# A hybrid encoder layer on one core: the order of the first stage's loads, x blocks and first products

## The chip, the cores and the metric

The kernel runs on one core of a Trainium2 chip. TensorE (PE) multiplies matrices and transposes, VectorE (DVE) and ScalarE (ACT) work elementwise, GpSimd (POOL) does small vector work, and SyncE's queue (SP) asks for most transfers. Each engine takes its own instructions in order and waits on semaphores for the others. The metric is the device time of one execution in microseconds; of several runs the median is given.

## What is computed

One layer of a streaming encoder, for a prompt of 512 frames and a sample of 64 frames, with width D = 2048, all in fp32:

```
mod = silu(c) @ w_ada + b_ada;  sh1, sc1, g1, sh2, sc2, g2 = split(mod, 6)
h = rmsnorm(x, norm1) * (1 + sc1) + sh1
proj = h @ w_in          # columns of GLA (q, k, v, r, low rank) and of DeltaNet (q, k, v, g, beta, alpha)
mix = [gated linear attention | gated DeltaNet](proj) @ w_out
x = x + g1 * mix
h = rmsnorm(x, norm2) * (1 + sc2) + sh2
x = x + g2 * (silu(conv3(gate) + b) * val @ w_down),  gate, val = split(h @ w_up)
y = rmsnorm(x, final_norm)
```

The DeltaNet part needs for each head and block the decays exp(cumsum(g)) with g from the alpha columns, and the inverse of a unit triangular 64 x 64 matrix. New states are returned too.

## The kernel before

Activations are kept transposed: 16 k-tiles of 128 features by two halves of 288 frames (256 of the prompt and 32 of the sample). For fp32 products each operand is split into two parts, high and low, and `mm6` (L555, matmuls at L564 and L566) makes six matmuls for one k-tile and one column of 128 weights: high by high, low by high, high by low, each for both halves. A column's sum lies in a PSUM tile named g, of which there are two (`pgt`, L579).

`head` (from L654) is the first stage. Its parts:

- The constants and small vectors are loaded and transposed (`load_vectors`, L593, transposes at L625).
- `modulation(g)` (L710) makes scale (mi = 1) and shift (mi = 0) for four k-tiles: for each, four chunks of four k-tiles of w_ada, of which each comes in two loads of 512 KB into tiles named hraw (five buffers, L720), with eight matmuls on quarters of the array (L724; two of them count as one step k). It ends with a copy from PSUM (L727), transposes (L157), a reduction (L730). It is a generator; each `yield` stands before a chunk.
- `x_block(b)` (L681) loads one block of x (four of the prompt, one of the sample), takes squares on ACT (L688), the norm by a power on POOL (L1725), scales on DVE (L692), transposes on PE (L697) and copies on ACT into xT (L700, L704). The five blocks are called between the chunks of modulation(0).
- Then for each group g of four k-tiles: the narrow weights (66 columns of low rank, beta, alpha, `narrow_w`) are loaded; four h tiles are made by `split_mod` (scale and shift on DVE at L586, high part hh on ACT at L587, low part hl on DVE at L588); each has four narrow products (L878); then come six columns (EARLY) of the in projection, in pairs by `pair_w` (L771: two loads of 256 KB each into a raw tile, high part on ACT at L778, low part on DVE at L779), and for each column four mm6 and `sum_early` (first group a copy on ACT, L788; later an addition on DVE, L793). modulation(g + 1) moves on by one step after each narrow product and each column.

When `head` is done, `narrow` (L880) starts the gate chain: the narrow sums are copied out (na) and turned (L891), beta and the logarithm ln follow on ACT and DVE, two products with a triangle of ones (L926) give cum, further ones (L935, L951) the last values and rows, which go through DRAM (gd, L954) and come back broadcast to all partitions (gb, L349). From this the decays are made, POOL selects the triangles, and together with keys (kt, norm on POOL at L1725) the matrix m, whose 16 x 16 blocks go through DRAM (d, L372 and L378) to POOL's inverse (`inverse16`, L367). PE meanwhile goes on with further columns of the in projection by mm6; L249, L255 and L157 are PE's later uses of that chain.

The order of the work is set by a scheduler of the framework: the program is written in one sequence, a priority can be raised in a block (`high_priority`, used in `pair_w`), and each engine then gets its fixed queue. Loads all stand on SP, in order, and each waits for its buffer. Buffers are reused in rotation (`bufs`), by which a load or product waits for the last reader.

## Time and profile before

| | us |
|---|---|
| median of 3 runs | 2925.44 (2918.93 to 2926.12) |
| the profiled execution | 2921.86 |
| its span | 2920.1 |
| first mm6 product (timeline) | 65.81 |
| last product of the head ends (chain) | 193.25 |
| POOL's first inverse starts (timeline) | 237.19 |

In the profile, L12 is a line of the kernel; "x6" counts instructions in a row, and "[1.40 <-ACT hh L587]" says that the engine stood idle for 1.40 us and that ACT's writing of hh ended it. "PEclk" is the clock granted to PE, in tenths. A group's row in the view by lines gives the busy time in total and the mean of one in ns. The waits of an engine are listed with their total, their number and the longest. DMA rows give what moved in a stretch.

### The profile page before, as it was taken

What the parts mean: (1) busy time and instruction counts of PE and PEld (TensorE: products, weight loads), DVE (VectorE), ACT (ScalarE), POOL (GpSimd) and SP (SyncE); (2) the same over time, 40 slices, a digit from 0 to 9 for tenths busy, and PEclk for the clock granted to TensorE, in tenths of its full rate; (3) what the DMA queues carried; (4) which work ended last, traced back from release to release, by engine and by line L of the source; (5) the groups of instructions that cost most, each with busy time, mean ns of one, the idle gap of its engine ahead of it and who ended that gap; (6) DMA issues with size and microseconds to landing.
All of it is one profiled execution on the core that took longest, in us unless ns stands there. A gap on an engine that the chain in (4) does not pass through costs nothing.

```text
span 2920.1 us, 52016 instructions
## 1 busy us (share of the span) xinstructions
PE 2823.8 (97%) x20964; PEld 2734.4 (94%) x20964; DVE 2051.2 (70%) x3299; ACT 1182.5 (40%) x2032; POOL 311.7 (11%) x513
## 2 busy tenths in 40 slices
PE   6999989999899999999999999999999999999998
PEld 3688889999899998999999999999999999999997
DVE  3368666777568787578888888888888855555555
ACT  4234534555454343255444444444444421222223
POOL 0005141222200000000111111111111100000000
PEclk8999999999999999999999999999999999999999
DMA  8865544555444548633333334333333553323221
GB/s 267 283 204 150 161 133 138 149 150 161 135 131 144 155 118 231 184 119 96 106 111 107 102 104 116 109 99 107 109 109 106 181 185 97 119 96 120 80 81 66
DMA packets 535444, 395.53 MB, mean 135 GB/s; under 512 B 59657, under 2 KB 465412, under 8 KB 535204
## 3 DMA queue, kind: packets, MB, share of 16 engines
q1 hardware_dynamic: 527860, 390.54, 44.7%
q8 instruction: 165, 2.70, 0.4%
q10 hardware_dynamic: 7344, 1.67, 0.3%
q14 instruction: 75, 0.61, 0.1%
HBM read 356.47 MB, written 35.67 MB: 134 GB/s over the span
## 4 chain that ended last, share of the span: by engine, by line
PE 80%; DVE 6%; POOL 4%; issue 4%; DMA 3%; ACT 2%; SPq 1%; ACTq 0%; POOLq 0%; DVEq 0%
PE g L564 26%; PE g L566 13%; PE bank L1388 11%; PE bank L1387 11%; PE bank L1389 11%; POOL m L1725 3%; DVE acc L850 1%; PE bank L724 1%; PE bank L157 1%; PE bank L441 1%; DVE wl L652 1%; DVE ca L990 1%; DVE m L1710 1%; ACT m L1710 1%; DMA d<-m 1%
## 5 line engine op out<-in xcount | busy, mean ns | idle before, releaser
L1388 PE MATMUL bank<-slot,wh 128*128 128x290 f32 x2464 | 737.3, 299 | 0.0
L1387 PE MATMUL bank<-slot,wh 128*128 128x290 f32 x2464 | 733.2, 298 | 0.0
L1389 PE MATMUL bank<-slot,wl 128*128 128x290 f32 x2464 | 728.2, 296 | 0.0
L564 PE MATMUL g<-slot,wh 128*128 128x288 f32 x3168 | 552.7, 295 | 0.2 <-DVE slot L1157 0.2
L564 PE MATMUL g<-hh,wh 128*128 128x288 f32 x2048 | 476.6, 313 | 1.0 <-ACT wh L651 1.0
L1389 PEld LDWEIGHTS bank<-slot,wl 128*128 128x128 f32 x2464 | 470.6, 191 | 0.0
L1388 PEld LDWEIGHTS bank<-slot,wh 128*128 128x128 f32 x2464 | 468.7, 190 | 0.1
L564 PEld LDWEIGHTS g<-slot,wh 128*128 128x128 f32 x3168 | 464.5, 188 | 0.7 <-DVE slot L1157 0.5
L1387 PEld LDWEIGHTS bank<-slot,wh 128*128 128x128 f32 x2464 | 463.6, 188 | 0.1
L651 ACT ACTIVATE wh<-raw 128x1024 fp32r<-128x1024 f32 x215 | 227.6, 1058 | 539.1 <-PE g L564 507.0
L564 PE MATMUL g<-hl,wh 128*128 128x288 f32 x2048 | 445.1, 298 | 0.0
L566 PE MATMUL g<-hh,wl 128*128 128x288 f32 x2048 | 443.7, 297 | 0.0
L1157 DVE SCALAR_TENSOR_TENSOR slot<-g,mod,slot 128x512 f32<-128x512 f32 (+1 forms) x448 | 201.6, 491 | 268.5 <-PE g L566 267.7
L564 PEld LDWEIGHTS g<-hh,wh 128*128 128x128 f32 x2048 | 328.4, 191 | 20.8 <-issue 16.3
L850 DVE SCALAR_TENSOR_TENSOR acc<-aw,ct,acc 128x512 f32<-128x512 f32 x480 | 337.7, 750 | 10.2 <-DMA aw<-in_w_ada_dram 10.2
L566 PE MATMUL g<-slot,wl 128*128 128x288 f32 x1584 | 342.6, 295 | 0.0
L566 PEld LDWEIGHTS g<-hh,wl 128*128 128x128 f32 x2048 | 331.6, 190 | 6.2 <-issue 6.2
L564 PEld LDWEIGHTS g<-hl,wh 128*128 128x128 f32 x2048 | 332.4, 190 | 3.6 <-issue 3.5
L652 DVE TENSOR_TENSOR wl<-raw,wh 128x1024 fp32r<-128x1024 f32 x215 | 262.6, 1222 | 64.6 <-ACT wh L651 64.0
L1334 ACT ACTIVATE wh<-raw 128x1024 fp32r<-128x1024 f32 x176 | 186.2, 1058 | 224.2 <-PE bank L1388 182.3
L566 PEld LDWEIGHTS g<-slot,wl 128*128 128x128 f32 x1584 | 256.1, 188 | 0.0
L1335 DVE TENSOR_TENSOR wl<-raw,wh 128x1024 fp32r<-128x1024 f32 x176 | 215.3, 1223 | 54.0 <-ACT wh L1334 54.0
(351 smaller groups left out, 3102.2 us busy)
## 6 DMA issues: line engine op xcount, KB each, us to landing
raw<-in_w_up_dram SPq DMA_DIRECT2D x176, 512.0 KB
aw<-in_w_ada_dram SPq DMA_DIRECT2D x128, 512.0 KB
raw<-in_w_in_dram SPq DMA_DIRECT2D x100, 512.0 KB
raw<-in_w_down_dram SPq DMA_DIRECT2D x88, 512.0 KB
hraw<-in_w_ada_dram SPq DMA_DIRECT2D x64, 512.0 KB
raw<-in_w_out_dram SPq DMA_DIRECT2D x32, 512.0 KB
slot<-actd SPq DMA_DIRECT2D x44, 288.0 KB
actd<-v SPq DMA_DIRECT2D x44, 256.0 KB
```

Of the source, the lines that this page charges most:

```text
L564: T.matmul(ps[:, h if bank is None else bank, :n], wh, x[:, h, :n], start=f, stop=False)
L566: T.matmul(ps[:, h if bank is None else bank, :n], wl, ah[:, h, :n], start=False, stop=stop)
L651: nc.scalar.activation(hi[:, :n_], raw[:, :n_], AF.Copy)
L652: nc.vector.tensor_tensor(lo[:, :n_], raw[:, :n_], hi[:, :n_].bitcast(F32), op=ALU.subtract)
L850: V.scalar_tensor_tensor(acc[s], w[:, k], col, acc[s], op0=ALU.mult, op1=ALU.add)
L1157: self.nc.vector.scalar_tensor_tensor(x1[:, :, z], ps[:, :, c], gain[:, q:q + 1], x1[:, :, z], op0=ALU.mult, op1=ALU.add)
L1334: self.nc.scalar.activation(hi, src, AF.Copy)
L1335: self.nc.vector.tensor_tensor(lo, src, hi.bitcast(F32), op=ALU.subtract)
L1387: T.matmul(ps, wh[:, j], hi, start=(c < 3 and j == 0), stop=False, skip_group_check=True)
L1388: T.matmul(ps, wh[:, j], lo, start=False, stop=False, skip_group_check=True)
L1389: T.matmul(ps, wl[:, j], hi, start=False, stop=(j == NPAIR - 1), skip_group_check=True)
L1725: r = f(*a, **kw)
```

## The change

The diff, cut to its core (load_vectors is split into its loads and its transposes in the same way; line numbers move by 1 to 30 in head and by 87 or 88 behind it, so L564 is L565, L724 is L754, L878 is L966, L926 is L1014, L935 is L1023, L1725 is L1812):

```diff
+N_HRAW, HRAW_AHEAD = 8, 3
...
-    def split_mod(self, x, s, b, hh, hl, tmp):
+    def split_mod(self, x, s, b, hh, hl, tmp, other=False):
 
         nc = self.nc
         for c, q in ((slice(0, HP), 0), (slice(HP, HT), 1)):
+            if other:
+                nc.scalar.activation(tmp[:, :, c], x[:, :, c], AF.Identity, bias=b[:, q:q + 1], scale=s[:, q:q + 1])
+                continue
             nc.vector.tensor_scalar(tmp[:, :, c], x[:, :, c], s[:, q:q + 1], b[:, q:q + 1], op0=ALU.mult, op1=ALU.add)
...
+        def x_load(b):
+            n = P if b < 4 else TS
+            xt[b] = [slot() for _ in range(4)]
+            for q in range(4):
+                f = slice(q * 512, (q + 1) * 512)
+                nc.sync.dma_start(xt[b][q][:n], i["x_prompt"][0, b * P:(b + 1) * P, f] if b < 4 else i["x_sample"][0, :, f])
+
+        def x_square(b):
+            n = P if b < 4 else TS
+            ms[b] = pool.tile([P, 8], F32, tag="ms4", bufs=2, name=self.name("ms4"))
+            for q in range(4):
+                A.activation(junk[:n], xt[b][q][:n], AF.Square, scale=float(D) ** -0.5, accum_out=ms[b][:n, q:q + 1])
+
+        def x_scale(b):
+            n, m = P if b < 4 else TS, ms[b]
+            V.tensor_reduce(m[:n, 4:5], m[:n, 0:4], axis=mybir.AxisListType.X, op=ALU.add)
+            self.rsqrt(m[:, 5:6], m[:, 4:5], 1, n)
+            for q in range(4):
+                V.tensor_scalar_mul(xt[b][q][:n], xt[b][q][:n], m[:n, 5:6])
+
+        def x_turn(b):
+            n = P if b < 4 else TS
+            per = 4 if b < 4 else 8
+            for k0 in range(0, KD, per):
+                ps = self.pgt()[:, 0]
+                for k in range(k0, k0 + per):
+                    T.transpose(ps[:, (k - k0) * n:(k - k0 + 1) * n], xt[b][k // 4][:n, k % 4 * P:(k % 4 + 1) * P],
+                                self.c["ident"][:n, :n])
+                even = k0 // per % 2 == 0
+                put = (lambda o, x: A.activation(o, x, AF.Copy)) if even else V.tensor_copy
+                if b < 4:
+                    put(xT[:, k0:k0 + per, b // 2, (b % 2) * P:(b % 2 + 1) * P], ps.rearrange("p (k t) -> p k t", k=per))
+                else:
+                    for h in range(2):
+                        put(xT[:, k0:k0 + per, h, HP:HT], ps.rearrange("p (k h t) -> p k h t", k=per, h=2)[:, :, h])
+
+        junk = slot()
+        x_load(0)
+        x_load(1)
+        self.load_consts(self.cp, LONG)
+        v_load, v_turn = self.load_vectors()
+        v_load(0)
+        v_load(1)
+        x_load(2)
+        v_turn(0)
+        v_turn(1)
...
-        def x_block(b):
-            n = P if b < 4 else TS
...
-        hraw = self.hraw = lambda: pool.tile([P, 1024], F32, tag="hraw", bufs=5, name=self.name("hraw"))
+        hraw = self.hraw = lambda: pool.tile([P, 1024], F32, tag="hraw", bufs=N_HRAW, name=self.name("hraw"))
+        todo = [(g, mi, k0) for g in range(4) for mi in (1, 0) for k0 in range(0, KD, 4)]
+        got = {}
+
+        def ada_ahead(n):
+            for j in range(len(got), min(n, len(todo))):
+                g, mi, k0 = todo[j]
+                c0 = mi * D + g * 512
+                got[j] = [hraw().rearrange("p (k n) -> p k n", k=2) for _ in range(2)]
+                for h, raw in enumerate(got[j]):
+                    k1 = k0 + 2 * h
+                    nc.sync.dma_start(raw, i["w_ada"][0, k1 * P:(k1 + 2) * P, c0:c0 + 512].rearrange("(k p) n -> p k n", p=P))
 
         def modulation(g):
+            for n in range(8 * g, 8 * g + 8):
+                _, mi, k0 = todo[n]
+                ada_ahead(n + 1)
+                if k0 == 0:
+                    ps = self.bank()
+                for k in (2, 3, 0, 1):
+                    with self.tc.issue_after(last) if k == 0 else nullcontext():
+                        T.matmul(ps[32 * k:32 * k + 32], cs[:, k0 + k], got[n][k // 2][:, k % 2], start=(k0 == 0), stop=(k0 == KD - 4))
+                    last = nc.cur_bb.bb.instructions[-1]
+                got[n] = None
+                ada_ahead(n + 1 + HRAW_AHEAD)
+                if k0 + 4 < KD:
                     yield
+                    continue
                 rw = pool.tile([P, 512], F32, tag="rw", bufs=1, name=self.name("rw"))
                 V.tensor_copy(rw, ps)
+                if g > 0:
+                    yield
...
+                if mi == 1:
+                    self.scale_mod(s1, 1, "norm1", 4 * g)
+
+        first = modulation(0)
+        ada_ahead(1)
+        x_load(3)
+        ada_ahead(2)
+        x_load(4)
+        for g in (2, 3, 4):
+            v_load(g)
+        late = [lambda: v_turn(2), lambda: v_turn(3), lambda: v_load(5), lambda: v_turn(4), lambda: v_load(6), lambda: v_turn(5), lambda: v_turn(6)]
+        for b in range(5):
+            if b == 0:
+                x_square(0)
+            x_scale(b)
+            if b < 4:
+                x_square(b + 1)
+            x_turn(b)
+            if b > 0:
+                next(first)
+        for _ in first:
+            pass
+
+        pairs = [(g, e) for g in range(4) for e in range(0, len(EARLY), 2)]
+        self.h, raws = [], {}
+
+        def w_ahead(n):
+            for j in range(len(raws), min(n, len(pairs))):
+                g, e = pairs[j]
+                raws[j] = self.pair_load([off + h * P for _, off, h in EARLY[e:e + 2]], 4 * g)
+
+        w_ahead(2)
...
+        def make(k):
+            hh, hl = self.htiles(k)
+            tmp = pool.tile([P, 2, HT], F32, tag="tmp", bufs=2, name=self.name("tmp"))
+            self.split_mod(xT[:, k], s1[:, k], self.mod[:, 0, k], hh, hl, tmp, k in (1, 3))
+            self.h.append((hh, hl))
+
+        nar = self.narrow_w(pool, 0)
         for g in range(4):
             mods = modulation(g + 1) if g < 3 else iter(())
             ks = range(4 * g, 4 * g + 4)
-            nar = self.narrow_w(pool, 4 * g)
-            for k in ks:
-                hh, hl = self.htiles(k)
-                tmp = pool.tile([P, 2, HT], F32, tag="tmp", bufs=2, name=self.name("tmp"))
-                self.split_mod(xT[:, k], s1[:, k], self.mod[:, 0, k], hh, hl, tmp)
-                self.h.append((hh, hl))
-                self.mm_narrow(k, nar[:, k % 4])
-                next(mods, None)
-            if g == 3:
-                raw = self.xr()
-                self.ps_nar = raw[:, :2 * HT].rearrange("p (h t) -> p h t", h=2)
-                V.tensor_copy(self.ps_nar[:64], ps_nar[:64, :, :HT])
-            for e in range(len(EARLY)):
-                if e % 2 == 0:
-                    w = self.pair_w([off + h * P for _, off, h in EARLY[e:e + 2]], 4 * g)
-                wh, wl = w[e % 2]
-                ps = self.pgt()
-                for k in ks:
-                    self.mm6(ps, wh[:, k % 4], wl[:, k % 4], self.h[k], k == 4 * g, k == 4 * g + 3)
-                self.sum_early(e, g, ps, accs[e])
-                next(mods, None)
+            for e in range(0, len(EARLY), 2):
+                w = self.pair_split(raws[3 * g + e // 2])
+                ps = [self.pgt() for _ in range(2)]
+                if e == 0:
+                    for k in ks:
+                        if k == len(self.h):
+                            make(k)
+                        self.mm_narrow(k, nar[:, k % 4])
+                        for j in range(2):
+                            self.mm6(ps[j], w[j][0][:, k % 4], w[j][1][:, k % 4], self.h[k], k == 4 * g, k == 4 * g + 3)
+                        if k == ks[1]:
+                            w_ahead(3 * g + 3)
+                        next(mods, None)
+                        if late:
+                            late.pop(0)()
+                    if g == 3:
+                        raw = self.xr()
+                        self.ps_nar = raw[:, :2 * HT].rearrange("p (h t) -> p h t", h=2)
+                        V.tensor_copy(self.ps_nar[:64], ps_nar[:64, :, :HT])
+                    for j in range(2):
+                        self.sum_early(j, g, ps[j], accs[j])
+                    continue
+                for j in range(2):
+                    if e == 4 and g < 3 and j == 0:
+                        nar = self.narrow_w(pool, 4 * g + 4)
+                    for k in ks:
+                        if e == 4 and g < 3 and j == 1 and k % 2 == 0:
+                            make(4 * g + 4 + k % 4 // 2)
+                        self.mm6(ps[j], w[j][0][:, k % 4], w[j][1][:, k % 4], self.h[k], k == 4 * g, k == 4 * g + 3)
+                        if k % 2 == 1:
+                            next(mods, None)
+                        if k == ks[1]:
+                            if late:
+                                late.pop(0)()
+                            if j == 0:
+                                w_ahead(3 * g + e // 2 + 3)
+                    self.sum_early(e + j, g, ps[j], accs[e + j])
...
+    def pair_load(self, offs, k0):
+
+        raw = self.raw()
+        for e, off in enumerate(offs):
+            self.nc.sync.dma_start(raw[:, e * 512:(e + 1) * 512].rearrange("p (k n) -> p k n", k=4), self.w_in(off)(k0, k0 + 4))
+        return raw
...
-        K.load_consts(K.cp, LONG)
```

What it does, in the order of the program:

- x blocks 0 and 1 are asked for ahead of the constants and vectors, block 2 behind the first vectors, 3 and 4 around chunk 1 of w_ada. The other vectors' loads and transposes move back, some into the columns (`late`).
- The block's work is cut into load, square, scale and turn; the squares of block b + 1 stand ahead of the transposes of block b, and the copies into xT alternate between ACT and DVE.
- hraw has eight buffers in place of five, and up to four chunks are asked for ahead of use.
- The loads of w_in pairs are apart from their splits and are asked for two to three pairs ahead.
- Within a group the first two columns run side by side: for each k-tile the narrow products and the products of both columns. The h tiles of the next group's first two k-tiles are made in the last column of this group. For k-tiles 1 and 3 of the first group ACT makes the scaled tile too.

Three places in the engines' queues. SP, where the first pair of w_in (raw) is asked for. Before:

```order
L685 DMA hs_461<-in_x_sample_dram 64x512
L685 DMA hs_462<-in_x_sample_dram 64x512
L720 DMA hraw_501<-in_w_ada_dram 128x2x512
L777 DMA raw_619<-in_w_in_dram 128x4x128
L720 DMA hraw_502<-in_w_ada_dram 128x2x512
L777 DMA raw_619<-in_w_in_dram 128x4x128
L720 DMA hraw_509<-in_w_ada_dram 128x2x512
L720 DMA hraw_510<-in_w_ada_dram 128x2x512
L720 DMA hraw_517<-in_w_ada_dram 128x2x512
L720 DMA hraw_518<-in_w_ada_dram 128x2x512
L867 DMA hraw_543<-in_w_in_dram 128x4x16 x2
```

and now:

```order
L744 DMA hraw_499<-in_w_ada_dram 128x2x512
L744 DMA hraw_500<-in_w_ada_dram 128x2x512
L744 DMA hraw_507<-in_w_ada_dram 128x2x512
L744 DMA hraw_508<-in_w_ada_dram 128x2x512
L744 DMA hraw_515<-in_w_ada_dram 128x2x512
L744 DMA hraw_516<-in_w_ada_dram 128x2x512
L858 DMA raw_529<-in_w_in_dram 128x4x128 x2
L858 DMA raw_532<-in_w_in_dram 128x4x128 x2
L955 DMA hraw_542<-in_w_in_dram 128x4x16 x2
L744 DMA hraw_583<-in_w_ada_dram 128x2x512
```

The first pair (raw_619 before, raw_529 now) stood within chunk 5 (counted from 0) and now stands behind chunk 10.

PE, where the second group of k-tiles begins (g is a column's sum, bank the sum of w_ada, ps_nar the narrow sum). Before:

```order
L564 MATMUL g_832<-hl_601,wh_781 128x288 x2
L566 MATMUL g_832<-hh_600,wl_782 128x288 x2
L878 MATMUL ps_nar<-hh_865,nar_859 66x288 x2
L724 MATMUL bank_876<-hraw_889,cs 32x512 x2
L724 MATMUL bank_876<-hraw_888,cs 32x512
L878 MATMUL ps_nar<-hl_866,nar_859 66x288 x2
L878 MATMUL ps_nar<-hh_877,nar_859 66x288 x2
L878 MATMUL ps_nar<-hl_878,nar_859 66x288 x2
L724 MATMUL bank_876<-hraw_888,cs 32x512
L564 MATMUL g_941<-hh_865,wh_935 128x288 x2
L564 MATMUL g_941<-hl_866,wh_935 128x288 x2
```

and now:

```order
L565 MATMUL g_811<-hl_661,wh_806 128x288 x2
L567 MATMUL g_811<-hh_660,wl_807 128x288 x2
L565 MATMUL g_901<-hh_858,wh_897 128x288 x2
L565 MATMUL g_901<-hl_859,wh_897 128x288 x2
L567 MATMUL g_901<-hh_858,wl_898 128x288 x2
L565 MATMUL g_902<-hh_858,wh_897 128x288 x2
L565 MATMUL g_902<-hl_859,wh_897 128x288 x2
L567 MATMUL g_902<-hh_858,wl_898 128x288 x2
L754 MATMUL bank_919<-hraw_756,cs 32x512 x2
L754 MATMUL bank_919<-hraw_755,cs 32x512 x2
L565 MATMUL g_901<-hh_877,wh_897 128x288 x2
```

The narrow products stood first and now stand behind the first k-tiles' products of both columns, g_901 and g_902.

PE in the columns behind the head, where the gate chain's products with ln and cum stand (g_1853 and g_1994 are the first two such columns). Before:

```order
L564 MATMUL g_1853<-hl_1193,wh_1919 128x288 x2
L566 MATMUL g_1853<-hh_1192,wl_1920 128x288
L926 MATMUL bank_1815<-ln,xr_1768 128x32
L927 MATMUL bank_1815<-ln,xr_1768 128x4
L566 MATMUL g_1853<-hh_1192,wl_1920 128x288
L564 MATMUL g_1853<-hh_1211,wh_1919 128x288 x2
L564 MATMUL g_1853<-hl_1212,wh_1919 128x288 x2
L566 MATMUL g_1853<-hh_1211,wl_1920 128x288 x2
L564 MATMUL g_1853<-hh_1230,wh_1919 128x288 x2
L935 MATMUL bank_1824<-cum,xr_1768 128x36
L936 MATMUL bank_1824<-cum,xr_1768 128x4
L951 MATMUL bank_1842<-consts_96,cum 36x128
```

and now:

```order
L565 MATMUL g_1994<-hh_955,wh_1996 128x288 x2
L565 MATMUL g_1994<-hl_956,wh_1996 128x288
L1014 MATMUL bank_1815<-ln,xr_1768 128x32
L1015 MATMUL bank_1815<-ln,xr_1768 128x4
L565 MATMUL g_1994<-hl_956,wh_1996 128x288
L567 MATMUL g_1994<-hh_955,wl_1997 128x288 x2
L565 MATMUL g_1994<-hh_986,wh_1996 128x288 x2
L565 MATMUL g_1994<-hl_987,wh_1996 128x288 x2
L1023 MATMUL bank_1824<-cum,xr_1768 128x36
L1024 MATMUL bank_1824<-cum,xr_1768 128x4
L1039 MATMUL bank_1842<-consts_193,cum 36x128
L567 MATMUL g_1994<-hh_986,wl_1997 128x288 x2
```

These products stood in the first column and now stand in the second.

71 lines of the change are left out of this document (13 added, 58 removed).

## The prediction

> **What bounds the kernel now.** I read the page first: its span, the engines' totals, the clock by slices and the shares by line of the chain that ended last.
>
> ```profile
> span 2920.1 us, 52016 instructions
> PE 2823.8 (97%) x20964; PEld 2734.4 (94%) x20964; DVE 2051.2 (70%) x3299; ACT 1182.5 (40%) x2032; POOL 311.7 (11%) x513
> PEclk8999999999999999999999999999999999999999
> PE g L564 26%; PE g L566 13%; PE bank L1388 11%; PE bank L1387 11%; PE bank L1389 11%; POOL m L1725 3%; DVE acc L850 1%; PE bank L724 1%; PE bank L157 1%; PE bank L441 1%; DVE wl L652 1%; DVE ca L990 1%; DVE m L1710 1%; ACT m L1710 1%; DMA d<-m 1%
> ```
>
> PE is busy 97% of the span, so time can be won only where PE waits or runs slowly; the clock is lowest in the first slice. POOL's 3% of the chain says that PE also waits for POOL somewhere. The change rewrites the first stage, so I read that next: as a timeline (start, length, instruction, and in brackets the idle time before it), in 5 us windows (columns: busy us of PE, PEld, DVE, ACT, POOL; granted clock; DMA share; GB/s), and its transfers up to 66 us.
>
> ```profile
> 10.16 0.63 ACT L688 ACTIVATE hs<-hs 128x512 f32<-128x512 f32 x1 [5.64 <-DMA hs<-in_x_prompt_dram]
> 14.14 0.55 POOL L1725 TENSOR_TENSOR ms<-ms,mhalf 128x1 f32<-128x1 f32 x1 [11.84 <-DVE ms L150]
> ...
> 47.42 0.54 POOL L1725 TENSOR_TENSOR ms<-ms,mhalf 64x1 f32<-64x1 f32 x1 [7.33 <-DVE ms L150]
> ...
> 50.60 0.66 ACT L704 ACTIVATE xT<-g 128x256 f32<-128x256 f32 x2 [0.19 <-PE g L697]
> ...
> 65.81 0.53 PE L564 MATMUL g<-hh,wh 128*128 128x288 f32 x2
> ...
> 71.62 0.43 PE L564 MATMUL g<-hh,wh 128*128 128x288 f32 x2
> 71.88 0.43 PE L564 MATMUL g<-hl,wh 128*128 128x288 f32 x2
> ```
>
> ```profile
> 15.00:20.00 5.00, 4.73 (x24) 3.21 (x24) 1.40 (x4) 3.22 (x7) 0.00 (x0) 1.00 1.05 406
> 50.00:55.00 5.00, 4.13 (x22) 0.96 (x20) 1.23 (x1) 2.00 (x5) 0.00 (x0) 0.52 0.28 68
> 60.00:65.00 5.00, 4.30 (x15) 2.07 (x16) 4.86 (x12) 2.73 (x4) 0.00 (x0) 0.50 0.99 318
> ```
>
> ```profile
> DMA packets 12526, 17.63 MB, mean 267 GB/s; under 512 B 1948, under 2 KB 4723, under 8 KB 12522
> hraw<-in_w_ada_dram SPq DMA_DIRECT2D x23, 512.0 KB
> ```
>
> Before the first product (65.81) the five x blocks follow one another: POOL's norm of the first is at 14.14, of the fifth at 47.42, which is 8.3 us each, and x is in place at 51.3. DMA can move 406 GB/s, yet its mean up to 66 us is 267, and 68 at 50:55: the five w_ada buffers are full and wait to be used. From 65.81 on PE is the bound, with holes only where a group of four h tiles begins (waits of PE from 65.8 to 194; total, times, longest; then the rows of the last hole):
>
> ```profile
> PE ps_nar L878 <- ACT hh L587: 4.9, 3, 2.3
> PE ps_nar L878 <- DVE hl L588: 0.8, 1, 0.8
> ```
>
> ```profile
> 171.15 0.74 PE L878 MATMUL ps_nar<-hl,nar 128*66 128x288 f32 x2 [0.76 <-DVE hl L588]
> ...
> 172.65 0.68 PE L566 MATMUL g<-hh,wl 128*128 128x288 f32 x2
> 173.13 0.68 PE L564 MATMUL g<-hh,wh 128*128 128x288 f32 x2
> ...
> 174.70 0.43 PE L564 MATMUL g<-hl,wh 128*128 128x288 f32 x2
> ```
>
> That is 5.7 us of waiting, and behind the last hole pairs start 0.48 apart (172.65, 173.13) where 0.26 is usual (71.62, 71.88): half clock from 170.9 to 174.3, 1.7 us lost. The head ends with the last product at 193.25 (the chain), and behind it stand the gate chain and the first inverse on POOL:
>
> ```profile
> 193.25 0.99 PE bank L891 x8
> ```
>
> ```profile
> 209.28 0.33 SPq L349 DMA_DIRECT2D m<-gd  x1
> 216.89 3.04 POOL L1725 TENSOR_SCALAR_AFFINE_SELECT m<-m 128x512 f32<-128x512 f32 x2 [110.49 <-ACT m L1710]
> 223.85 1.35 POOL L1725 TENSOR_TENSOR kt<-kt,mhalf 128x4 f32<-128x4 f32 x1 [3.92 <-PE bank L227]
> 237.19 0.12 POOL L1725 MEMSET m<- 32x16 f32 x1 [8.44 <-DMA m<-d]
> ```
>
> ```profile
> PE bank L157 <- DVE m L1710: 6.4, 1, 6.4
> PE bank L255 <- POOL m L1725: 6.1, 1, 6.1
> ```
>
> From 190 to 340 PE loses 12.5 us in waits on what this chain feeds. So what PE wins before 193.25 only lengthens these waits, unless the chain starts earlier too. That makes its start the second term of the sum.
>
> **The change, part by part.** No arithmetic goes away: products, transposes and loads keep their number. I use these groups (busy us, mean ns):
>
> ```profile
> L779 DVE TENSOR_TENSOR wl<-raw,wh 128x1024 fp32r<-128x1024 f32 x12 | 14.7, 1224 | 6.9 <-ACT wh L778 6.9
> L793 DVE SCALAR_TENSOR_TENSOR acc<-g,acc 128x576 f32<-128x576 f32 x17 | 12.9, 757 | 33.9 <-PE g L566 33.7
> L588 DVE TENSOR_TENSOR hl<-tmp,hh 128x576 fp32r<-128x576 f32 x16 | 11.6, 757 | 0.5
> L700 ACT ACTIVATE xT<-g 128x512 f32<-128x512 f32 x16 | 9.2, 594 | 13.2 <-PE g L697 12.8
> L727 DVE COPY rw<-bank 128x512 f32<-128x512 f32 x8 | 5.5, 692 | 36.9 <-PE bank L724 36.9
> ```
>
> *x first, overlapped.* x0 is asked for ahead of the constants, so its squares start some 4 us sooner than 10.16. The next block's squares run beside a block's transposes, and four copies on two engines take 2 x 0.69 in place of 4 x 0.59, 1 us less. I take 7 us a block in place of 8.3: x is in place at 51.3 - 4 - 5 x 1.3 = 41 at the latest, and I expect 38 to 41. The Trainium skill ("VectorE: DVE Perf Modes", Specifications) says that VectorE sits closer to SBUF and ScalarE closer to PSUM, which speaks against copies from PSUM by VectorE. The two rows agree (692 against 594), and by it alone the moved copies would cost 10 x 0.1 = 1 us; side by side they still win more.
>
> *Loads.* SP now asks for chunks 8 to 10 of w_ada (1.05 MB each, two of the 512 KB rows) ahead of the first w_in pair. Chunk 7 on needs buffers that PE frees once x is turned, near 39. Four chunks and the pair (4.7 MB) at 375 GB/s, a little under the best window, take 12.5 us, to 52 with a landing. Split on ACT and DVE (1.06 and 1.22), h tiles and narrow products put the first product at 58, 7.8 us sooner. Bounds: 54 (406 GB/s, x at 38) and 62 (318 GB/s, x at 41).
>
> *First product to head's end*, 127.4 us now. A product takes 0.133 (two rows 0.26 to 0.27 apart, two in each). Removed: waits 5.7, half clock 1.7, and of 28 runs of w_ada products (five chunks are split in two runs) five, at 1.18 each, 5.9. Added: eight narrow products that stood ahead of the first product, 1.2; half clock at the start, since PE idles between 42 and 57, 1.6. 127.4 - 5.7 - 1.7 - 5.9 + 1.2 + 1.6 = 116.9. The h tiles made early are hidden by the last column's 3.2 us of products; without that cover the old holes return.
>
> *A new wait.* Two columns side by side hold both g tiles. The second column needs the sum (0.757) of the column before, covered by the first column's six products (0.8); the third column likewise at the other end. Eight joints: at best nothing, at worst the sum stands behind a split and an hl on DVE, 0.76 + 1.22 + 0.76 - 0.8 = 1.9 each, 15 in all. DVE waited 33.7 us for PE at L793, so it is mostly early: I take 0.2 each, 1.6.
>
> Head's end: 58 + 116.9 + 1.6 = 176.5, 16.7 us sooner.
>
> *The gate chain.* Of the next columns' products, 60 stood ahead of ln's (8.0 us), now 136 do (18.1). cum, the trip through gd and the selects follow, 10.1 later against PE's work. POOL stood idle 3.92 ahead of kt, whose product on PE hasn't moved: that is the slack, and the inverse comes 10.1 - 3.9 = 6.2 later. One us more for ln, which PE may reach before it is ready, makes 7.2. Bounds: 2 (from gd's read to the selects passed 7.6 us, half of it in other work's queues, which may shrink by 4) and 11 (no slack). PE's order behind is the same, so what the inverse loses stays to the end.
>
> **Sum.** -16.7 + 7.2 = -9.5. The profiled execution took 2921.86, 1.8 over its span, so 2912.4 on its own terms. The median of the runs is 2925.44, 3.6 higher; on it 2915.9, which I predict. 0.3% (8.8 us) is about what a measurement can tell from no change.
>
> The Trainium skill ("DMA: Bandwidth & Descriptors", Specifications) gives about 358 GB/s as one core's limit on HBM. The 406 of 15:20 is above it, so the measurement decides; by that figure the 4.7 MB would take 13.1 us and the estimate be 0.6 later.
>
> **Rivals.**
> *The start gains little and is given back* (0.27). Loads bound the start after all: first product at 62, the chain 11 later: -12.7 + 11 = -1.7, 2923.7. For it: 318 at 60:65, with DMA busy 0.99; against: 406 at 15:20.
> *The chain isn't later* (0.15). If queues shrink around it as in the lower bound or more, 1 in place of 7.2: -15.7, 2909.7. The place of ln's product speaks against it.
> *Slower by the g tiles* (0.13). Sums behind a split and both of ACT's and DVE's h tiles (0.76 + 1.22 + 2 x 0.76 - 0.8 = 2.7) at eight joints are 21.6, less the 1.6 taken: +10.5, 2935.9. It decides from 1.4 us a joint on. For it: DVE takes its queue in order. Against: the 33.7.
>
> **Chances.** My case has 0.45 and its own range 2911 to 2921; 0.30 of it lies beyond 0.3%. With 0.14 of the unchanged chain and 0.02 of the first rival's better end that is 0.46 faster; slower 0.11, nearly all of it the g tiles; within 0.43. The range reaches to the first two rivals with the ends of their terms: 2907 to 2928.
>
> **What would show it.** x's last copy by 41; first product near 58; no wait on hh or hl at L966; waits on DVE for the sums under 0.5 each; head's end near 176.5; POOL's first inverse near 237.2 - 9.5 = 227.7; waits of PE for POOL's and DVE's m about 20 in place of 12.5. An inverse at 237 or later means no gain, one at 221 the whole gain.

## The result and the profile after

| | before | after |
|---|---|---|
| median of 7 runs, us | 2924.99 (2918.93 to 2927.18) | 2915.48 (2912.49 to 2916.33) |
| the profiled execution, us | 2921.86 | 2915.48 |
| its span, us | 2920.1 | 2913.8 |

After to before is 0.997, with an interval of 0.9961 to 0.998; by the medians 9.5 us are won. The two profiled executions differ by 6.4 us only, since that of before lies 3.1 under the median of its seven and that of after on its median. Where the traces are compared below, about 6 us are to be found, not 9.5. One of the 19 executions of before that e9 to e12 below share took 10211.82 us at a granted clock of 0.527; it stands in none of their ratios.

The page of after: span, engines, granted clock.

```profile
span 2913.8 us, 52011 instructions
PE 2823.6 (97%) x20964; PEld 2739.5 (94%) x20964; DVE 2055.0 (71%) x3305; ACT 1183.4 (41%) x2030; POOL 306.1 (11%) x513
PEclk8998999999899999999999999999999999999999
```

PE is as busy as before in us (2823.6 against 2823.8), with the same number of matmuls, and the span is shorter: what was won is idle time of PE. Next the timeline of after up to the first product, then its 5 us windows (columns: busy us of PE, PEld, DVE, ACT, POOL; granted clock; DMA share; GB/s).

```profile
4.08 0.63 ACT L689 ACTIVATE hs<-hs 128x512 f32<-128x512 f32 x1 [2.00 <-DMA hs<-in_x_prompt_dram]
...
28.84 21.05 SPq L744 DMA_DIRECT2D hraw<-in_w_ada_dram  x18
...
40.89 3.35 PE L754 MATMUL bank<-hraw,cs 128*32 128x512 f32 x16
40.99 0.76 DVE L712 COPY xT<-g 128x256 f32<-128x256 f32 x2 [0.93 <-PE g L704]
...
50.16 7.14 SPq L858 DMA_DIRECT2D raw<-in_w_in_dram  x4
...
51.47 1.94 PE L754 MATMUL bank<-hraw,cs 128*32 128x512 f32 x8 [2.59 <-DMA hraw<-in_w_ada_dram]
...
61.46 1.04 ACT L866 ACTIVATE wh<-raw 128x1024 fp32r<-128x1024 f32 x1
...
62.55 0.85 PE L565 MATMUL g<-hh,wh 128*128 128x288 f32 x2 [0.39 <-ACT wh L866]
```

```profile
35.00:40.00 5.00, 0.98 (x9) 1.01 (x10) 2.59 (x7) 2.22 (x7) 0.54 (x1) 0.70 1.05 406
40.00:45.00 5.00, 4.24 (x25) 1.36 (x24) 1.47 (x4) 0.66 (x2) 0.00 (x0) 0.62 0.39 125
45.00:50.00 5.00, 3.58 (x28) 0.99 (x28) 0.56 (x4) 0.00 (x0) 0.00 (x0) 1.00 1.01 351
50.00:55.00 5.00, 2.69 (x12) 0.92 (x12) 0.69 (x1) 0.00 (x0) 0.00 (x0) 0.56 1.04 399
55.00:60.00 5.00, 3.45 (x17) 0.83 (x19) 3.50 (x11) 3.03 (x6) 0.00 (x0) 0.75 1.09 379
```

x's first squares start at 4.08 in place of 10.16, and x's last copies at 40.99, which puts x in place at 41.8 in place of 51.3. The first product is at 62.55, only 3.3 us earlier. Between lies a hole of the transfers: at 40:45 they move 125 GB/s, since the buffers of w_ada come free only with PE's run of 16 products from 40.89 on (SP asks for chunk 6 at 42.85). Then they run at 351 to 399 GB/s. SP's queue holds w_ada until 49.9, and the first pair of w_in is asked for at 50.16, behind it. PE's chunk 7 waits for its load (51.47). The first h tiles need its shift, and the pair is split behind them in ACT's queue, at 61.46. ACT's row there shows no wait for the pair, so the first product hangs on chunk 7.

Behind the first product, PE's waits from 55 to 185 that touch the columns, and those from 185 to 340:

```profile
PE ps_nar L966 <- ACT hh L591: 1.4, 1, 1.4
PE g L565 <- ACT wh L866: 0.4, 1, 0.4
PE ps_nar L966 <- DVE hl L592: 0.3, 1, 0.3
```

```profile
PE bank L256 <- DVE m L1797: 7.5, 1, 7.5
PE bank L256 <- POOL m L1812: 3.9, 1, 3.9
PE bank L250 <- DVE m L399: 2.8, 1, 2.8
PE bank L1014 <- DVE ln L1012: 1.0, 1, 1.0
PE bank L910 <- DVE acc L938: 0.9, 1, 0.9
```

The 5.7 us at the groups' boundaries are 1.7 now, and no wait of PE for a column's sum g appears. Behind the head the waits on what the gate chain feeds have grown from 12.5 us (12.7 with 0.2 at L249) to 14.2 (7.5, 3.9 and 2.8). The windows show both sides at once, first of before, then of after:

```profile
65.00:185.00 120.00, 114.38 (x782) 84.37 (x781) 51.16 (x97) 26.74 (x35) 0.64 (x2) 0.99 0.84 259
185.00:330.00 145.00, 131.66 (x993) 128.78 (x993) 104.87 (x203) 73.49 (x174) 46.39 (x71) 0.95 0.53 157
```

```profile
65.00:185.00 120.00, 118.17 (x851) 93.84 (x850) 54.98 (x102) 27.19 (x37) 1.10 (x3) 1.00 0.78 256
185.00:330.00 145.00, 128.76 (x950) 125.15 (x949) 105.58 (x209) 76.43 (x177) 40.95 (x71) 0.94 0.55 157
```

In the head PE is busy for 3.8 us more, and behind it for 2.9 us less. To follow this through all kernels I use two places that are fixed in PE's queue: the first transposes of qkv (called A) and the transposes of rows behind the first inverses (called B). In each kernel of this text 1210 matmuls stand ahead of A and 1918 ahead of B (counted in the traces). A third product moves between them: ln's (L926 before, L1014 now) had 1086 matmuls ahead of it and now has 1162. In before, then in after:

```profile
203.14 0.41 PE L926 MATMUL bank<-ln,xr 128*128 128x32 f32 x2 [0.63 <-DVE ln L924]
...
219.47 0.60 PE L157 MATMUL bank<-consts,qkv 128*128 128x128 f32 x4
...
326.47 0.38 PE L157 MATMUL bank<-consts,rows 128*128 128x128 f32 x2
```

```profile
201.96 0.41 PE L1014 MATMUL bank<-ln,xr 128*128 128x32 f32 x2 [0.99 <-DVE ln L1012]
...
208.16 0.60 PE L158 MATMUL bank<-consts,qkv 128*128 128x128 f32 x4
...
320.65 0.38 PE L158 MATMUL bank<-consts,rows 128*128 128x128 f32 x2
```

A comes 11.3 us earlier, B 5.8 us: of what the start and the head win, 5.5 us is given back between A and B. ln's product stood 16.3 us ahead of A and now stands 6.2 us ahead of it, so the gate chain starts 10.1 us later against PE's other work. Of the 5.5 us, 2.5 are idle time of PE between A and B (15.2 against 12.7), and 3.0 are busy time of the same products (97.2 against 94.3) at a granted clock of 0.92 in place of 0.94. B's 5.8 is nearly the whole of the 6.4 between the two executions.

### The profile page after: what moved, and what is told of

Its sections match the earlier page's. It is cut to its first block, busy times and chain, and to the rows that moved or that the text cites. A ratio compares the mean times of both kernels' runs of the same rounds, so it can differ in the third digit from the quotient of the medians.

```text
span 2913.8 us, 52011 instructions
## 1 busy us (share of the span) xinstructions
PE 2823.6 (97%) x20964; PEld 2739.5 (94%) x20964; DVE 2055.0 (71%) x3305; ACT 1183.4 (41%) x2030; POOL 306.1 (11%) x513
## 4 chain that ended last, share of the span: by engine, by line
PE 83%; DVE 6%; POOL 3%; issue 2%; DMA 2%; ACT 2%; SPq 0%; ACTq 0%; POOLq 0%; DVEq 0%
PE g L565 28%; PE g L567 14%; PE bank L1476 12%; PE bank L1475 11%; PE bank L1477 11%; POOL m L1812 2%; DVE acc L938 2%; PE bank L754 1%; PE bank L158 1%; PE bank L442 1%; DVE m L1797 1%; DVE wl L663 1%; DVE ca L1078 1%; ACT m L1797 0%; PE bank L256 0%
## 5 line engine op out<-in xcount | busy, mean ns | idle before, releaser
L565 PE MATMUL g<-slot,wh 128*128 128x288 f32 x3168 | 551.4, 295 | 0.3 <-DVE slot L1245 0.3
L565 PE MATMUL g<-hh,wh 128*128 128x288 f32 x2048 | 478.6, 314 | 1.3 <-ACT wh L662 0.8
L565 PEld LDWEIGHTS g<-slot,wh 128*128 128x128 f32 x3168 | 464.1, 188 | 0.7 <-DVE slot L1245 0.5
L565 PE MATMUL g<-hl,wh 128*128 128x288 f32 x2048 | 444.9, 298 | 0.0
L565 PEld LDWEIGHTS g<-hh,wh 128*128 128x128 f32 x2048 | 329.8, 192 | 25.5 <-issue 14.9
L565 PEld LDWEIGHTS g<-hl,wh 128*128 128x128 f32 x2048 | 333.7, 191 | 3.6 <-issue 2.7
```

Source lines behind the costliest of these rows:

```text
L565: T.matmul(ps[:, h if bank is None else bank, :n], wh, x[:, h, :n], start=f, stop=False)
```

## The experiments

The kernels e1 to e4, e5 to e8 and e9 to e12 each shared their executions of the kernel before. The table has the first mm6 product, how far ln's product stands ahead of A, A, and B less A (all from the timelines, us), PE's busy us from 65 to 185 and from 185 to 330 (windows), and the time: median, median of before beside it, ratio with interval. Per kernel there is one trace, and its execution isn't always near the median. From B to its end a trace takes between 2591.0 us (e6) and 2599.4 us (e9), so a few us at B are easily lost in the time.

| | first product | ln to A | A | B - A | PE busy, head, behind | median | before | ratio |
|---|---|---|---|---|---|---|---|---|
| before | 65.81 | 16.3 | 219.47 | 107.0 | 114.4, 131.7 | | | |
| after | 62.55 | 6.2 | 208.16 | 112.5 | 118.2, 128.8 | 2915.48 | 2924.99 | 0.997 (0.9961 to 0.998) |
| e1 seven buffers | 65.44 | 16.3 | 209.97 | 108.0 | 118.2, 132.8 | 2916.22 | 2927.32 | 0.9962 (0.9949 to 0.9974) |
| e2 pair early | 59.56 | 6.2 | 212.35 | 112.6 | 116.4, 128.6 | 2923.18 | 2927.32 | 0.9989 (0.9981 to 0.9998) |
| e3 both | 63.46 | 16.3 | 216.60 | 107.6 | 116.4, 132.2 | 2920.16 | 2927.32 | 0.9974 (0.9963 to 0.9985) |
| e4 start only | 65.32 | 16.5 | 209.08 | 106.8 | 117.4, 131.9 | 2912.70 | 2927.32 | 0.995 (0.9938 to 0.9962) |
| e5 eight, less memory | 66.60 | 16.4 | 215.35 | 107.7 | 115.1, 133.0 | 2917.97 | 2924.57 | 0.9978 (0.997 to 0.9987) |
| e6 start only, eight | 66.31 | 16.3 | 212.34 | 107.0 | 116.0, 132.9 | 2912.04 | 2924.57 | 0.9961 (0.9947 to 0.9974) |
| e7 start, x as before | 64.81 | 16.3 | 207.93 | 108.3 | 118.0, 132.6 | 2912.03 | 2924.57 | 0.996 (0.9948 to 0.9973) |
| e8 start, copies by ACT | 66.06 | 16.3 | 209.67 | 107.4 | 117.4, 131.7 | 2913.59 | 2924.57 | 0.9966 (0.9953 to 0.9978) |
| e9 x as before, five | 64.43 | 16.3 | 216.02 | 108.7 | 114.6, 131.1 | 2918.22 | 2927.23 | 0.9967 (0.9957 to 0.9977) |
| e10 columns only | 64.72 | 17.6 | 219.47 | 106.1 | 114.3, 131.3 | 2917.91 | 2927.23 | 0.9976 (0.9967 to 0.9985) |
| e11 chunks before turns | 67.47 | 16.3 | 211.20 | 106.9 | 117.0, 133.1 | 2913.57 | 2927.23 | 0.9961 (0.9948 to 0.9975) |
| e12 no early tiles | 65.11 | 16.3 | 210.65 | 107.8 | 117.1, 132.3 | 2914.36 | 2927.23 | 0.996 (0.9947 to 0.9972) |

**e1: seven buffers for w_ada.**

```diff
-N_HRAW, HRAW_AHEAD = 8, 3
+N_HRAW, HRAW_AHEAD = 7, 3
```

> Seven hraw buffers in place of eight, the order of the loads up to the first product unchanged. With eight, the copies of the narrow sums (na) stand behind all of the last group's sums on DVE and the gate chain's product with ln behind 136 products of the next columns; with seven they stand right behind the copy out of PSUM and ln's behind 60, as before the change. Theory G (the eighth buffer's memory holds na back, and the chain's later start is the second term of the sum): head's end near 181.5 as after the change, POOL's first inverse 6 us earlier than its 231.2, near 225, and the time 5 to 7 us under the changed kernel, about 2909. Theory S (running two columns side by side delays the narrow sums, whatever the memory): inverse and time as after the change, 231 and 2915.

One buffer less (4 KB in each partition), and the gate chain is back in its place: ln's product is 16.3 us ahead of A as before, and B - A is 108.0. The copy of the narrow sums (na), with which the chain begins, shows where it was held. DVE's rows in after, then in e1, with ln's product:

```profile
167.12 0.75 DVE L832 COPY xr<-ps_nar 64x576 f32<-64x576 f32 x1 [0.59 <-PE ps_nar L966]
...
183.94 0.41 DVE L973 COPY na<-xr 64x512 f32<-64x512 f32 x1
```

```profile
169.25 0.75 DVE L832 COPY xr<-ps_nar 64x576 f32<-64x576 f32 x1 [0.57 <-PE ps_nar L966]
...
170.59 0.41 DVE L973 COPY na<-xr 64x512 f32<-64x512 f32 x1
...
193.68 0.41 PE L1014 MATMUL bank<-ln,xr 128*128 128x32 f32 x2 [0.65 <-DVE ln L1012]
```

In after the narrow sums are ready at 167.9, yet na is written at 183.94, when the head is through; in e1 it follows 0.6 us behind the sums (170.0). na, the constants of this part and the gate tiles lie in a pool of their own, which shares SBUF with the head's pool and takes over its tiles one by one as they are done with. With eight buffers na has to wait for a tile that the head uses to its end. That the pools share an address is read from the program; that memory, and not the order of the columns, decides the chain's place is shown by this run and by e5. The time doesn't tell e1 from after. Of the 4.5 us of B - A that the chain wins, 1.8 are lost by a later A, as the first product is 2.9 us later. B is 2.7 us earlier (317.98 against 320.65), but the spans of the two traces agree (2914.0 and 2913.8), and so do the ratios within their intervals.

**e2: the first pairs and narrow weights asked for behind chunk 5.**

```diff
         for b in range(5):
+            if b == 4:
+                w_ahead(2)
+                nar = self.narrow_w(pool, 0)
...
-        w_ahead(2)
...
-        nar = self.narrow_w(pool, 0)
```

> The changed kernel, but the first two w_in pairs and the narrow weights are asked for behind chunk 5 of w_ada in place of chunk 10. Theory L (the first product waits for its weights, which stand behind chunks 8 to 10): first product at 58 to 59 in place of 62.6, head's end 3 to 4 us earlier than 181.5; the gate chain still late. Time 2912, as far as the chain lets it through. Rival P (chunk 7 and the h tiles are as late as the pair): first product at 61 or later, time 2915 as after the change.

The first product comes at 59.56, the earliest of all, 3.0 us ahead of after, and the kernel is the slowest of the changed ones: 2923.18, with an interval (0.9981 to 0.9998) above that of after. The pair took the place of w_ada in SP's queue, so 184 of the 256 products of w_ada are left behind the first product, as before, in place of 168 (counted in the traces). The waits at the boundary of groups are longer than in after (1.4 and 0.3):

```profile
PE ps_nar L967 <- ACT hh L591: 2.2, 1, 2.2
PE ps_nar L967 <- DVE hl L592: 0.8, 1, 0.8
```

PE is busy for 1.8 us less than in after from 65 to 185, and A is 4.2 us later. PE has the same work to do in either order, and an early first product that leaves more of w_ada for later won nothing here.

**e3: both, seven buffers and the early pair.** The edits of e1 and of e2 together.

> Seven buffers and the early pair together. If G and L hold and their gains add: first product 58 to 59, head's end near 178, inverse near 222, time 2905 to 2907. If the two are not independent (the chain hides the head again): time within 2 us of the seven buffers alone.

The chain is in its place (16.3, 107.6), but A is 8.4 us later than in after, and the time is 2920.16. The two edits don't add up to a gain. In the trace the early pair costs 6.6 us at A beside e1, more than the 4.5 that the chain wins; in time e3 can't be told from after (0.9974 and 0.997).

**e4: the start alone.** Seven buffers, columns one after another, no h tiles made early.

```diff
-N_HRAW, HRAW_AHEAD = 8, 3
+N_HRAW, HRAW_AHEAD = 7, 3
...
                         self.mm_narrow(k, nar[:, k % 4])
-                        for j in range(2):
-                            self.mm6(ps[j], w[j][0][:, k % 4], w[j][1][:, k % 4], self.h[k], k == 4 * g, k == 4 * g + 3)
...
                     for j in range(2):
+                        for k in ks:
+                            self.mm6(ps[j], w[j][0][:, k % 4], w[j][1][:, k % 4], self.h[k], k == 4 * g, k == 4 * g + 3)
                         self.sum_early(j, g, ps[j], accs[j])
...
-                        if e == 4 and g < 3 and j == 1 and k % 2 == 0:
-                            make(4 * g + 4 + k % 4 // 2)
```

> The first part of the change alone, on seven buffers: x first and overlapped, loads ahead, but each group's columns one after another and its h tiles made when the group begins. Theory: the columns' part is worth 5.7 us of waits and 1.7 of half clock at the group boundaries, of which the changed kernel shows 1.7 left, so 5 to 6 us later at the head's end than with seven buffers, and about 2914. Rival: the boundary waits are covered by the loads asked for ahead, so that the time is within 2 us of the seven buffers, about 2910.

2912.70, a ratio of 0.995 (0.9938 to 0.9962): the best ratio of all kernels, and it meets that of after (0.9961 to 0.998) only at the ends of the intervals. Beside e1 it differs in the columns alone, and is not slower without them. The waits that the columns were to take away have not come back; of e4's waits from 55 to 185:

```profile
PE ps_nar L964 <- ACT hh L591: 2.0, 1, 2.0
PE ps_nar L964 <- DVE hl L592: 0.5, 1, 0.5
```

That is 2.5 us against 5.7 before and 1.7 in after. The loads further ahead and the cut of load and split are still in e4; e9 and e10 tell which of these counts.

**e5: eight buffers, with room made elsewhere.** The scaled tile and the narrow weights get one buffer each.

```diff
-            tmp = pool.tile([P, 2, HT], F32, tag="tmp", bufs=2, name=self.name("tmp"))
+            tmp = pool.tile([P, 2, HT], F32, tag="tmp", bufs=1, name=self.name("tmp"))
...
-        s = pool.tile([P, 4, NW], F32R, tag="nar", bufs=2, name=self.name("nar"))
+        s = pool.tile([P, 4, NW], F32R, tag="nar", bufs=1, name=self.name("nar"))
```

> The changed kernel with all eight hraw buffers, but the scaled tile tmp and the narrow weights with one buffer each in place of two, 3.3 KB of a partition less; ln's product then stands behind 60 products again. Theory G (memory of the first stage holds the gate chain back, whichever tile frees it): first product at 62.6 to 64, head's end within 1.5 us of the changed kernel's, no loss behind it, POOL's first inverse near 226, time 4 to 6 us under the changed kernel, about 2911 where the kernel before takes 2925. Rival B (it is the count of w_ada buffers, through the loads): the chain stays late and the time is as after the change.

The chain is back (16.4, 107.7) with eight buffers, the side-by-side columns and the early tiles all in place. So none of these moves it; the memory does. The price is elsewhere: with one scaled tile the first h tiles follow one another, and PE waits at the first product:

```profile
66.60 0.85 PE L565 MATMUL g<-hh,wh 128*128 128x288 f32 x2 [3.19 <-ACT wh L866]
```

A is 7.2 us later than in after, and the time 2917.97 is no better.

**e6: the start alone with eight buffers and e5's memory.** The columns of e4, the two edits of e5, and eight buffers.

> The start alone (columns one after another, h tiles made when the group begins), with eight hraw buffers and the same 3.3 KB saved. If the eighth buffer is worth the 3 us by which the first product came sooner in the changed kernel than with seven: first product near 62.5, time 2 to 3 us under the start alone with seven buffers, ratio to before near 0.994. Rival: PE must do the same w_ada products later anyway, so the first product is sooner but the head's end is not, and the ratio stays at 0.995.

2912.04, with the chain in its place. Its A is 3.3 us later than e4's and its ratio overlaps with e4's; an eighth buffer, together with the single tiles that make room for it, adds nothing that shows. Beside e5, which differs in the columns alone, it is 5.9 us shorter in the same company, and the intervals (0.9947 to 0.9974, 0.997 to 0.9987) overlap a little: the side-by-side columns don't help here either.

**e7: the start alone, x as before.** e4, but constants and vectors are asked for ahead of x, x two blocks ahead, the squares follow the block before, and all copies are ACT's.

```diff
-                even = k0 // per % 2 == 0
-                put = (lambda o, x: A.activation(o, x, AF.Copy)) if even else V.tensor_copy
+                put = lambda o, x: A.activation(o, x, AF.Copy)
...
-        x_load(0)
-        x_load(1)
...
-        x_load(2)
...
-        x_load(3)
+        x_load(0)
         ada_ahead(2)
-        x_load(4)
+        x_load(1)
...
-            if b == 0:
-                x_square(0)
+            x_square(b)
             x_scale(b)
-            if b < 4:
-                x_square(b + 1)
             x_turn(b)
+            if b < 3:
+                x_load(b + 2)
```

> The start alone with seven buffers, but x as in the kernel before: constants and vectors asked for first, each block two blocks ahead at most, its squares behind the previous block's transposes, all copies on ACT. What is left is loads asked for ahead (seven buffers, three chunks ahead, pairs ahead). Theory X (x in place sooner is what the start gains): x's last copy near 50 in place of 42, head's end 5 to 8 us later than with x first, ratio near 0.998. Rival A (the chunks asked for ahead do it, and x hides behind them): head's end within 2 us, ratio near 0.995.

2912.03 (2911.02 to 2912.62): x first, overlapped and copied by two engines is worth nothing that can be measured. The timeline of e7 (chunk 7 is the run at 53.07):

```profile
47.67 0.66 ACT L706 ACTIVATE xT<-g 128x256 f32<-128x256 f32 x2 [0.23 <-PE g L704]
...
53.07 1.06 PE L750 MATMUL bank<-hraw,cs 128*32 128x512 f32 x8 [0.16 <-DMA hraw<-in_w_ada_dram]
...
63.70 1.06 ACT L859 ACTIVATE wh<-raw 128x1024 fp32r<-128x1024 f32 x1 [1.60 <-DMA raw<-in_w_in_dram]
...
64.81 0.54 PE L565 MATMUL g<-hh,wh 128*128 128x288 f32 x2 [1.18 <-ACT wh L859]
```

x is in place at 48.3, while in e4 its last copies start at 41.47, and the first product is not later (64.81 against 65.32). In e4 PE has x early, but waits for the loads of w_ada, and chunk 7 runs at 53.89. In e7 x comes 6 us later and PE reaches chunk 7 at 53.07, with its load just in place (0.16 us of waiting). Behind it the split waits 1.60 us for the first pair.

**e8: the start alone, all copies by ACT.** The first hunk of e7's diff on top of e4.

> The start alone with seven buffers, all copies into xT on ACT. By my term for the two engines (1 us a block): x's last copy 3 to 5 us later and the head's end 2 to 4 us later. By the rule that ACT is the nearer engine to PSUM (594 ns against 692) and if the copies hide behind the squares' and transposes' waits: x's last copy within 1 us and the time the same.

0.9966 against e4's 0.995, with intervals that overlap; A is 0.6 us and B 1.2 us later. Moving half of the copies to DVE may win a microsecond, and it is not shown. What the Trainium skill says of the engines' places ("VectorE: DVE Perf Modes", Specifications), from which the prediction drew a price for copies from PSUM by VectorE, is neither borne out nor refuted in time by this.

**e9: e7 with five buffers.**

```diff
-N_HRAW, HRAW_AHEAD = 7, 3
+N_HRAW, HRAW_AHEAD = 5, 1
```

> As the start alone with x as before, but with five hraw buffers and one chunk ahead, as the kernel before has them; what is left of the change is that w_in pairs are asked for apart from their split and ahead, and that the small vectors come later. Theory A (w_ada asked for further ahead is what the start gains): two chunks fewer done before the first product, head's end 4 to 6 us later than with seven buffers, ratio near 0.998. Rival W (the pairs asked for ahead do it): head's end within 2 us, ratio near 0.996.

What is left of the change here is chiefly the loads of pairs asked for ahead of their splits, the vectors' transposes moved back, and ACT's two scaled tiles. In the trace A is 8.1 us later than in e7. 184 products of w_ada are left behind the first product, in 23 runs, in place of 168 in 20, and PE's busy time in the head falls from e7's to about that of before; the windows of e7, then of e9:

```profile
65.00:185.00 120.00, 117.96 (x862) 96.12 (x862) 57.73 (x112) 28.82 (x39) 0.63 (x2) 0.99 0.84 270
```

```profile
65.00:185.00 120.00, 114.63 (x816) 89.92 (x815) 55.84 (x107) 29.12 (x41) 0.64 (x2) 0.97 0.85 270
```

The waits at the groups' boundaries are back as well. Of e9's waits from 55 to 185:

```profile
PE ps_nar L959 <- ACT hh L591: 2.1, 1, 2.1
PE g L565 <- ACT hh L591: 1.7, 2, 1.0
PE ps_nar L959 <- DVE hl L592: 0.5, 1, 0.5
```

That is 4.3 us in place of e7's 2.0, and e10, with the new columns and the early tiles on top, has some 4.5. So in the traces the loads of w_ada further ahead are what moves the head, and they also make 2.3 of the 3.7 us by which the boundary waits fell from before to e7. In time it is less plain: 2918.22 against 2912.03, but each against its own executions of before 0.9967 and 0.996, and the intervals overlap. e9's profiled execution took 2925.86, 7.6 over its median. In that trace B lies only 1.7 us ahead of B in before's, while e9's median is 9.0 us under that of before: what wins these 9 us isn't seen in the traces at hand, and stays open.

**e10: the columns alone.** e9 with columns side by side and early tiles.

> The same start with five buffers and x as before, with the change's columns: first two columns side by side, two h tiles made in the last column. My terms for the columns (5.7 us of waits and 1.7 of half clock at the group boundaries, against 1.6 of new waits) make it 3 to 6 us faster than the start with five buffers alone. Rival C, by the start alone being 2 to 3 us faster than the changed kernel with seven buffers: it is 0 to 3 us slower than that.

2917.91 against 2918.22 in the same company: the columns gain nothing. A (219.47) stands as in before and B (325.56) 0.9 us ahead of it, while the median lies 9.3 us under that of before: the same open question as with e9.

**e11: chunks ahead of the turns.** e4 with each chunk's products ahead of the block's transposes, and a chunk's loads one earlier among those of x.

```diff
-        x_load(2)
...
         ada_ahead(1)
-        x_load(3)
+        x_load(2)
         ada_ahead(2)
+        x_load(3)
+        ada_ahead(3)
         x_load(4)
...
+            next(first)
             x_turn(b)
-            if b > 0:
-                next(first)
```

> The start alone with seven buffers, w_ada asked for one chunk sooner among the x blocks, and each chunk's products emitted ahead of the x transposes instead of behind them, so that hraw buffers come free sooner. If the pauses of the loads (87 GB/s from 25 to 30 us in the changed kernel) are waits for buffers: first product 2 to 4 us sooner than the 65.4 of the start alone, and the time 2 to 4 us less, ratio near 0.994. If PE's order decides nothing there, or x comes later for it: the time as the start alone, 0.995.

A is 2.1 us later than in e4, the first product 2.2, and the ratio 0.9961 is no better. Drawing w_ada further forward in this way brings nothing that shows.

**e12: seven buffers, columns side by side, no early tiles.** e1 without the two lines of e4's last hunk.

> Seven buffers, the changed kernel's side by side columns, but the h tiles made when the group begins. If the early tiles are what costs the columns' part its gain (DVE and ACT work in the last column): the time falls to that of the start alone, ratio 0.995. If side by side does it: as the changed kernel with seven buffers, 0.996, or above it, since the boundary waits of 5 us come back.

2914.36, a ratio of 0.996 as e1's 0.9962. PE's waits at L964 are 2.8 us in place of e1's 1.7: the early tiles hide about a microsecond at the boundaries, which doesn't reach the time.

## Why the prediction came out

**The total** was right: -9.5 by the medians, as predicted. Much of this is luck. The sum was made on the profiled execution, and on the two traces it is -5.8 at B and -6.4 at the end; the rest comes from before's trace, an execution 3.1 us under its median, from which the prediction had counted up to the median. And e9, which has neither x first nor more buffers nor the new columns, wins about as much by its medians (0.9967 against 0.997). So the traces show the terms of the sum at work, with 5.8 us at B, but no time shows that they made the 9.5.

**The first product** is the term that was mis-sized: 58 predicted, 62.55 measured, -3.3 in place of -7.8, just past the bound of 62. x was in place at 41.8, little past the 38 to 41. The two steps behind it were too short. The buffers for chunk 7 and on were taken to come free near 39, but chunk 6 had to wait too, until 42.85: PE's products that free them stand behind the last transposes and run from 40.89 to 44.2 and on, and the transfers moved 125 GB/s at 40:45. So chunk 7 ran only at 51.47. And the work behind the loads was taken as 6 us, from the pair's landing at 52 to 58. It is 11.1 us, from chunk 7 through the shift, the h tiles and the split that stands behind them on ACT, to the first product. (By its own terms the prediction's lower bound is 56, not 54: x at 38 and 406 GB/s take 1 us each off 58.) The rate from 45 us on was right (351, 399 and 379 GB/s against the 375 assumed). e7 adds that an x in place 6 us later costs the first product nothing. The figure that the prediction set beside the rate, some 358 GB/s for one core in the Trainium skill ("DMA: Bandwidth & Descriptors", Specifications), is passed by the 406 of 35:40 and the 399 of 50:55.

**First product to head's end** was right. The chain of after has the products on na:

```profile
186.28 0.99 PE bank L979 x8
```

In PE's order 35 products of 0.133 now stand between the head's end and them, so the head ends near 181.6, and the term is 119.1 in place of 127.4, -8.3 (-8.9 predicted). Its parts moved against each other. The waits on hh and hl did not vanish, 1.7 of 5.7 remain, against "no wait on hh or hl". The joints of the g tiles cost nothing in place of 1.6, as DVE's 33.7 us of waiting had suggested. The runs of w_ada fell from 28 to 23, as forecast. But the reason given for the waits' fall, the early tiles and the side-by-side columns, was wrong for most of it: e4 has neither, and waits 2.5, while e10 has both, with five buffers, and waits some 4.5. The loads of w_ada further ahead make 2.3 of the 3.7 us from before to e7. (The eight narrow products at 0.133 are 1.1, not the 1.2 of the sum.)

**The head's end** was 176.5 predicted and is 181.6, by the first product's miss.

**The gate chain** was right in kind and near in size. ln's product stands 10.1 us later against PE's other work, just as predicted, and 5.5 us of it reach B (7.2 predicted, bounds 2 and 11). The first inverse starts at 231.20 (227.7 predicted, 237.19 before), 6.0 us earlier, which is B's gain. PE's waits for m are 14.2 us, not 20, and 1.0 for ln, as expected. The order told that the chain moves; it did not tell why, and the prediction didn't ask. The cause is the eighth buffer's memory (e1, e5). It could have been avoided, though no time shows a gain from that.

**The rivals.** Of "the start gains little and is given back" the first half came true (62.55 against 62), the second not: 5.5, not 11. "The chain isn't later" is refuted for this kernel, but is what e1 and e3 to e12 show. "Slower by the g tiles" is refuted: no wait on a sum.

**What gains.** Against before, the whole change in its present form wins 0.3%. Of its named parts, x first, overlap and copies by two engines show no gain (e7, e8), nor do the columns side by side (e4 beside e1, e10 beside e9) or the early tiles (e12). The loads of w_ada further ahead, with seven buffers, show in the traces (e7 beside e9, 8.1 us at A), but in time 0.996 and 0.9967 can't be told apart. What all changed kernels share (pairs asked for apart from their splits and ahead, the vectors' transposes moved back, ACT's two scaled tiles) is nearly all that e9 has, and e9's ratio is 0.9967. No run took these parts one by one, so which of them makes most of the gain isn't shown. The start alone with seven buffers (e4) is the best version by its ratio, 0.995.

## What to carry to other kernels

Measure a start at a product with a fixed place behind it, not at the first product: that of e2 came earliest, and e2 is the slowest of the changed kernels. When a buffer is added to a pool whose space another pool takes over, look in the new order for work of that other pool that has moved, since 4 KB held a copy back by 16 us (183.94, where the sums were ready at 167.9) and made the stretch from A to B some 5 us longer. And make the sum against a profiled execution that lies near the median, or say by how much it doesn't. A forecast that meets the median proves its terms only when a kernel without them misses it; e9 has few of them, and wins nearly as much.

## What was not expected of the hardware

The time of one and the same kernel often goes with its mean granted clock. Of the other 18 executions of before beside e9 to e12, the shortest took 2921.46 us at a granted clock of 0.987 and the longest 2931.03 at 0.983; of e9's nine, 2914.08 at 0.985 and 2925.86 at 0.979. It isn't so everywhere: e2's shortest and longest, 2920.98 and 2925.78, were at 0.984 and 0.985. In the trace of after, a long wait is followed by pairs of products at half pace (0.48 apart in place of 0.27):

```profile
286.88 1.94 PE L256 MATMUL bank<-m,m 128*128 128x64 f32 x8 [7.54 <-DVE m L1797]
...
289.20 0.68 PE L565 MATMUL g<-hl,wh 128*128 128x288 f32 x2
289.68 0.68 PE L567 MATMUL g<-hh,wl 128*128 128x288 f32 x2
...
294.26 0.43 PE L565 MATMUL g<-hh,wh 128*128 128x288 f32 x2
294.53 0.43 PE L565 MATMUL g<-hl,wh 128*128 128x288 f32 x2
```

The wait of 7.5 us thus costs some 3 us more behind it, by 6 us at half clock (a granted clock of 0.50 from 286.9 to 293). Whether such stretches make the spread between executions was not measured.
